# Attention with a bias on one core: ones column on GpSimd, a half-clock term in the emission planner, E tiles of twelve banks, and products of four banks

## The chip, the cores and the metric

The kernel runs on 1 core of a Trainium2 chip. The metric is the device time of one execution in microseconds (us); the number given for a kernel is the median over runs. Engines are named as in the profile: PE is TensorE (PEld its weight loads), DVE is VectorE, ACT is ScalarE, POOL is GpSimd, SP is SyncE.

## The reference

Batch 4, 8 heads, 1024 positions, head dimension 64, all float32, with one bias matrix of 1024 x 1024 for all heads:

```
scores = q @ k^T / sqrt(64) + bias
attn   = softmax(scores, axis=-1)        # denominator + 1e-8
out    = attn @ v
```

The inputs are small (normal draws times 0.1), so the kernel takes no maximum before the exponential.

## The kernel before

**Splitting the exponential.** exp(s + bias) is computed as exp(s) times exp(bias). ACT makes `eb` = exp(bias) once, from a bias transposed on PE (`b_fill`, L138, and `b_exp`, L143), and exp(s) for every head (`s_exp`, L130, into `E` tiles in bf16). DVE multiplies `E` by `eb` in place (`mul_pair`, L148). PE then multiplies the product with V (`av_bank`, L160). V has a 65th column of ones for every head and key block, in the tile `vall`, so that the same matmul gives the softmax denominator; the ones are written once, by a DVE memset (L200). An evacuation takes a reciprocal (L170) and scales (L171), and for the second half of the queries the output DMA follows on the SP queue (L174).

**The unit of work is a bank**: 128 keys by 512 queries of one head, one PSUM bank of scores. There are 16 pairs of heads, each with 2 query halves (`qh`), 8 key blocks (`kc`) and 2 heads: 512 banks, in this order, with the two heads of a pair alternating:

```python
banks = [(pr, h, qh, kc) for pr in range(NP) for qh in range(2) for kc in range(NCH) for h in range(2)]
slots = [[0], [1, 2]] + [list(range(i, min(i + 3, NB))) for i in range(3, NB, 3)]
```

A slot is what one exp instruction takes: 1, then 2, then 3 banks each, and 2 in the last. `s_fill` (L125) is the matmul of a slot, into one of two PSUM buffers of three banks (`ps_s`); so a fill can start when the exp two places earlier is done. Two more PSUM buffers (`ps_x`, tags xa and xb) serve the transposes of K and Q (L88, copied out by DVE at L101 and L97) and the accumulators of the V matmuls. A product of one key block covers the same `eb` block for the two heads. `E` tiles hold 6 banks, and there are 12 of them.

**The order of the work** is written out by a planner in Python. `order` fixes the sequence of ACT: the score slots, with four bias slots put in. For PE and DVE the planner keeps a model clock for each engine (`t_act`, `t_pe`, `t_dve`) with fixed costs in ns, `EXP` and `EXP0` for an exp, `QK` for a score matmul, `AV` for a bank of the V matmul, `TP` for eight transposes, `MUL` for a product, `COPYQ`, `COPYK` and `EVAC` for the other DVE work, and `SEM` for a hand-over, and emits whichever instruction its model has ready first. `pe_pick` lets other PE work go ahead of a fill only if it ends before a limit. The planner starts at the model time `T0`; what lies before (loads, the first transposes, slots 0 and 1) is written by hand. Engines run their instructions in the order in which they were emitted.

**The start.** SP and ACT load the first K chunks (`k0f`) and the first query half (`q0f`) in float32 by four small DMAs. POOL issues the other loads: the second halves of K and Q of pair 0, the first half of the bias, then V of pair 0 (L80, which waits for the ones memset because it writes the same tile), K and Q of pair 1 (L74, L75), the second half of the bias (L203), V of pair 1, and so on. PE is kept busy by six matmuls on zeros (L209). `k_first` (L213 cast, L217 transposes, L218 copy) and `q_first` (L221 cast, L224, L225) prepare the first K chunks and the first query half. After slot 2 the planner puts the transposes of the other K half and of the other query half of pair 0 (L88).

Of the kernel before, what the change touches and what calls it, by code (L numbers as in the profile page):

```python
# [11 lines left out]
ALU = mybir.AluOpType  # L12
# [3 lines left out]
def kernel(  # L16
# [15 lines left out]
    nc = tc.nc  # L32
    B, H, S, D = q.shape
    P = 128
    NCH = S // P
    D1 = D + 1
    NP = B * H // 2
    scale = 1.0 / (D ** 0.5)
    HQ = S // 2
# [8 lines left out]
    consts = ctx.enter_context(tc.tile_pool(name="consts", bufs=1))  # L48
    raw = ctx.enter_context(tc.tile_pool(name="raw", bufs=3))
    kvp = ctx.enter_context(tc.tile_pool(name="kvp", bufs=3))  # L50
    ep = ctx.enter_context(tc.tile_pool(name="ep", bufs=12))
    op = ctx.enter_context(tc.tile_pool(name="op", bufs=2))
    small = ctx.enter_context(tc.tile_pool(name="small", bufs=4))
    ps_s = ctx.enter_context(tc.tile_pool(name="ps_s", bufs=2, space=bass.MemoryType.PSUM))
# [5 lines left out]
    eb = consts.tile([P, 2, NCH, HQ], BF)  # L60
    mask = consts.tile([P, 2, HQ], BF)
    vall = consts.tile([P, 2 * NP, NCH, D1], BF)
# [42 lines left out]
    banks = [(pr, h, qh, kc) for pr in range(NP) for qh in range(2) for kc in range(NCH) for h in range(2)]  # L105
    NB = len(banks)
    slots = [[0], [1, 2]] + [list(range(i, min(i + 3, NB))) for i in range(3, NB, 3)]
    NS = len(slots)
    ET = 6
    etiles = {}  # L110

    def e_at(b, n):
        if b // ET not in etiles:
            etiles[b // ET] = ep.tile([P, ET, HQ], BF, name="E")
        return etiles[b // ET][:, b % ET:b % ET + n, :]

# [28 lines left out]
    def mul_pair(b, n=2):  # L145
        pr, h, qh, kc = banks[b]
        e = e_at(b, n)
        nc.vector.tensor_tensor(e, e, eb[:, qh, kc:kc + 1, :].to_broadcast([P, n, HQ]), op=ALU.mult)  # L148

    oalls = {}  # L150
    po = {}
# [25 lines left out]
    with tc.manual_schedule():  # L177
# [18 lines left out]
        for t in range(2):  # L196
            nc.vector.memset(qT0[t * D:(t + 1) * D, 1 - t, :HQ], 0.0)
            for u in range(2):
                nc.vector.memset(mask[t * D:(t + 1) * D, u, :], 1.0 if t == u else 0.0)
        nc.vector.memset(vall[:, :, :, D:D1], 1.0)  # L200
        load_v(0)
        load_qk(1)
        nc.gpsimd.dma_start(out=btraw[:, QC:, :], in_=bf_[:, QC:, :])  # L203
# [35 lines left out]

        EXP, EXP0, QK, AV, TP = 427, 45, 216, 170, 350
        MUL, COPYQ, COPYK, EVAC, SEM = 600, 650, 420, 620, 80
        order = [("S", g) for g in range(2, NS)]
        for at, x in ((5, (0, 0)), (7, (0, 4)), (11, (1, 0)), (13, (1, 4))):
            order.insert(at, ("B",) + x)
        NO = len(order)
        T0 = 7500.0
        t_act, t_pe, t_dve = T0 + 700, T0, T0 + 500
        filled = []  # L250
        act_end = []
        x_free = {"xa": T0 + 500, "xb": T0}
        x_unit = {}
# [6 lines left out]
        eb_at = {}  # L260
        exp_at = {0: T0, 1: T0 + 700, 2: T0 + 700}
        mul_at = {}
        mul_next = 0
# [9 lines left out]
            return banks[b][:3]  # L273

        dve_q = []

        def cost_act(i):
            item = order[i]
# [2 lines left out]
        def act_end_of(i):  # L281
            if i < 0:
                return T0
            if i < len(act_end):
                return act_end[i]
            return max(t_act, filled[i] + SEM if i < len(filled) else 0) + sum(
                cost_act(j) for j in range(len(act_end), i + 1))

        def pe_fill():
            i = len(filled)  # L290
            if i >= NO or i - 2 >= len(act_end):
                return None
            ready = act_end_of(i - 2) + SEM
            item = order[i]
            if item[0] == "S":
                for b in slots[item[1]]:
                    pr, h, qh, kc = banks[b]
                    for key in ((pr, 1, kc // QC), (pr, 0, qh)):
                        if key not in piece_end:
                            return None  # L300
                        ready = max(ready, piece_end[key] + SEM)
                cost = QK * len(slots[item[1]])
            else:
                ready = max(ready, bias_at[item[1]])
                cost = 2 * TP + 250

            def emit(t):
                if item[0] == "S":
                    s_fill(item[1])
                else:  # L310
                    b_fill(item[1], item[2])
                filled.append(t + cost)
            return ready, cost, emit

        def pe_piece():
            if not pieces:
                return None
            pr, which, half = pieces[0]
            if pr not in raw_at or pr not in raws:
                return None  # L320
            i = min(len(filled), NO - 1)
            while order[i][0] != "S":
                i -= 1
            at = slots[order[i][1]][0]
            if at < (pr - 2) * 32 + 8:
                return None

            left = NCH - av_next % NCH
            busy = x_unit.get(unit_of(av_order[av_next])) if av_next % NCH else None
            tags = sorted((x_free[x], x) for x in x_free if x != busy)  # L330
            if busy and left < 4 and at < pr * 32 - 16:
                return None
            if not busy and av_next and at < pr * 32 - 16 and tags[0][0] + SEM < t_pe and len(tags) > 1 and tags[1][0] > t_pe:
                return None
            free, tag = tags[0]
            ready = max(free + SEM, raw_at[pr][1 - which])

            def emit(t):
                pieces.pop(0)
                copy = transpose_pe(pr, which, half, tag)  # L340
                cost = COPYK if which else COPYQ
                x_free[tag] = 1e12

                def run(t2):
                    copy()
                    x_free[tag] = t2 + cost
                    piece_end[(pr, which, half)] = t2 + cost
                    if which == 0 and half == 1:
                        if pr + 3 < NP:
                            load_qk(pr + 3)  # L350
                            raw_at[pr + 3] = (t2 + 7000, t2 + 7000)
                        if pr + 2 < NP:
                            load_v(pr + 2)
                dve_q.append((t + TP + SEM, 0, cost, run))
            return ready, TP, emit

        def pe_av():
# [23 lines left out]
                    dve_q.append((t + AV + SEM, 1, EVAC, run))  # L381
            return ready, AV, emit

        def pe_pick():
            f = pe_fill()
            best = None
            i = len(filled)
            if f and f[0] <= t_pe:
                return (max(t_pe, f[0]),) + f[1:]
            limit = 1e12  # L390
            if f:
                limit = max(f[0], act_end_of(i - 1) - f[1] - 100)
            elif i < NO:
                limit = max(act_end_of(i - 2) + SEM, act_end_of(i - 1) - 750)
            for c in (pe_piece(), pe_av()):
                if c is None:
                    continue
                start = max(t_pe, c[0])
                if start + c[1] > limit:
                    continue  # L400
                if best is None or start < best[0]:
                    best = (start,) + c[1:]
            if f and (best is None or f[0] <= best[0]):
                best = (max(t_pe, f[0]),) + f[1:]
            return best

        def dve_pick():
            nonlocal mul_next
            c = list(dve_q)
            if mul_next < NB:  # L410
                pr, h, qh, kc = banks[mul_next]
                if mul_next + 1 in exp_at and (qh, kc) in eb_at:
                    b = mul_next

                    def run(t):
                        nonlocal mul_next
                        mul_pair(b)
                        mul_at[b] = mul_at[b + 1] = t + MUL
                        mul_next += 2
                    c.append((max(exp_at[b + 1], eb_at[(qh, kc)]) + SEM, 2, MUL, run))  # L420
            if not c:
                return None
            return min(c, key=lambda x: (max(x[0], t_dve + 100), x[1]))
# [7 lines left out]
        while len(act_end) < NO or av_next < NB or dve_q:  # L431
            c = []
            a, d, p = act_pick(), dve_pick(), pe_pick()
            if a:
                c.append((a[0], 0))
            if d:
                c.append((max(t_dve, d[0]), 1))
            if p:
                c.append((p[0], 2))
            t, who = min(c)  # L440
            if who == 0:
                i = a[2]
                item = order[i]
                t_act = t + a[1]
                act_end.append(t_act)
                if item[0] == "S":
                    s_exp(item[1])
                    for b in slots[item[1]]:
                        exp_at[b] = t_act
                else:  # L450
                    b_exp(item[1], item[2])
                    for kc in range(4):
                        eb_at[(item[1], item[2] + kc)] = t_act
            elif who == 1:
                if d in dve_q:
                    dve_q.remove(d)
                t_dve = t + d[2]
                d[3](t)
            else:
                t_pe = t + p[1]  # L460
                p[2](t)


# [28 lines left out]
```

## Time and profile before

| | us |
|---|---|
| median of 13 runs | 254.38 (253.3 to 255.29) |
| the profiled execution, its own time | 254.6 |
| span of its records | 252.8 |
| ACT busy | 239.1 |
| PE busy | 229.0 |
| DVE busy | 226.5 |
| POOL busy | 52.6 |

The span runs from the first to the last recorded instruction of the program; the time of the same execution is 1.8 us longer. Busy time is the union of an engine's records. On ACT and DVE the record of an instruction overlaps with that of the next by about 0.1 us to 0.4 us when they follow back to back, so the spacing of starts, not the mean of one record, is what an instruction costs there.

### The profile page before, as it was taken

How to read it: one execution, taken by the hardware profiler on the slowest of the kernel's cores; microseconds unless marked ns; L12 is line 12 of the kernel's file. 1: busy time of each engine (PE TensorE's matmuls, PEld its weight loads, DVE VectorE, ACT ScalarE, POOL GpSimd, SP SyncE). 2: the span in 40 equal slices, each digit the busy share in tenths (PEclk: the TensorE clock that was granted, in tenths of full speed). 3: DMA queues.
4: the chain of work that ended last, by engine and by line, in shares of the span. 5: the costliest groups of instructions: out<-in, count | busy, mean ns of one | idle time of the engine just before them, and what ended most of it. 6: DMA issues, size and time to landing. Idle time of an engine off the chain costs nothing.

```text
span 252.8 us, 7210 instructions
## 1 busy us (share of the span) xinstructions
PE 229.0 (91%) x3087; PEld 141.5 (56%) x3142; DVE 226.5 (90%) x461; ACT 239.1 (95%) x180; POOL 52.6 (21%) x72
## 2 busy tenths in 40 slices
PE   6769999999999999999999999999999999999982
PEld 2336755556555556565555556565565655555651
DVE  6309799999999999999999999999999999999994
ACT  3699999999999999999999999999999999999970
POOL 6653213513220513013042204034000000000000
PEclk9799999999999999999999999999999999999997
DMA  7999989989291589429196904949020201111112
GB/s 145 177 216 187 192 89 160 108 105 129 54 155 30 108 78 147 67 61 148 31 148 49 181 14 88 125 84 164 8 84 3 83 3 44 44 43 44 47 38 83
DMA packets 47743, 23.79 MB, mean 94 GB/s; under 512 B 34400, under 2 KB 43360, under 8 KB 47456
## 3 DMA queue, kind: packets, MB, share of 16 engines
q0 software_dynamic: 42272, 14.42, 53.3%
q1 hardware_dynamic: 5296, 8.78, 9.5%
q8 instruction: 24, 0.39, 0.7%
q10 hardware_dynamic: 144, 0.13, 0.2%
q14 instruction: 7, 0.06, 0.1%
HBM read 29.36 MB, written 8.39 MB: 149 GB/s over the span
## 4 chain that ended last, share of the span: by engine, by line
PE 45%; ACT 42%; DVE 8%; issue 2%; DMA 1%; ACTq 0%
ACT E L130 39%; PE ps L125 30%; PE po L160 9%; PE px L88 6%; DVE E L148 5%; ACT eb L143 3%; DVE oall L171 1%; DMA q0f<-in_q_dram 1%; DVE qT L97 1%; ACTq L130 0%; DVE rs L170 0%; DVE qT L225 0%; DVE kr L213 0%; DVE qr L221 0%; PE px L224 0%
## 5 line engine op out<-in xcount | busy, mean ns | idle before, releaser
L130 ACT ACTIVATE E<-ps 128x1536 bf16<-128x1536 f32 (+2 forms) x172 | 230.2, 1665 | 3.4 <-PE ps L125 3.4
L148 DVE TENSOR_TENSOR E<-E,eb 128x1024 bf16<-128x1024 bf16 x256 | 163.7, 683 | 8.0 <-ACT eb L143 7.8
L125 PE MATMUL ps<-qT,kT 128*128 128x512 bf16 x457 | 134.1, 380 | 11.9 <-ACT E L130 5.0
L160 PEld LDWEIGHTS <-E 128*128 128x128 bf16 x2048 | 84.5, 97 | 40.2 <-DVE E L148 2.5
L160 PE MATMUL po<-vall,E 128*128 128x65 bf16 x2048 | 96.3, 194 | 2.7 <-DVE E L148 1.3
L125 PEld LDWEIGHTS <-kT 128*128 128x128 bf16 x512 | 45.4, 97 | 42.2 <-issue 10.5
L74 POOL DMA_DIRECT2D kr<-in_k_dram x15 | 10.5, 699 | 98.5 <-PE px L88 95.4
L80 POOL DMA_DIRECT2D vall<-in_v_dram x32 | 28.1, 882 | 6.7 <-DMA btraw<-in_bias_dram 4.0
L171 DVE TENSOR_TENSOR oall<-po,rs 128x256 f32<-128x256 f32 x64 | 27.2, 425 | 2.4 <-DVE rs L170 0.3
L97 DVE TENSOR_TENSOR qT<-px,mask 128x1024 bf16<-128x1024 bf16 x31 | 21.3, 688 | 1.6 <-PE px L88 0.8
L101 DVE COPY kT<-px 128x512 bf16<-128x512 bf16 x31 | 13.1, 424 | 4.8 <-PE px L88 4.1
L170 DVE RECIPROCAL rs<-po 128x4 f32<-128x4 f32 x64 | 11.4, 178 | 3.4 <-PE po L160 3.1
L75 POOL DMA_DIRECT2D qr<-in_q_dram x15 | 10.7, 716 | 14.9 <-PE px L88 14.0
L88 PE MATMUL px<-ident,kr 128*64 128x128 bf16 x248 | 13.1, 227 | 0.3
L88 PE MATMUL px<-ident,qr 128*64 128x128 bf16 x248 | 13.0, 228 | 0.0
L88 PEld LDWEIGHTS <-kr 128*64 128x64 bf16 x248 | 8.1, 110 | 8.7 <-issue 5.2
L88 PEld LDWEIGHTS <-qr 128*64 128x64 bf16 x248 | 8.2, 111 | 7.6 <-issue 7.0
L143 ACT ACTIVATE eb<-pb 128x2048 bf16<-128x2048 bf16 x4 | 7.5, 1882 | 0.0
L138 PE MATMUL pb<-ident,btraw 128*128 128x128 bf16 x64 | 4.6, 225 | 1.8 <-ACT eb L143 1.0
L138 PEld LDWEIGHTS <-btraw 128*128 128x128 bf16 x64 | 4.6, 146 | 2.7 <-issue 2.4
L209 PE MATMUL wm<-zeros 128*128 128x512 bf16 x6 | 2.7, 629 | 1.2 <-DVE zeros L184 1.2
L185 ACT ACT_TABLE_LOAD x1 | 1.3, 1283 | 1.2 <-PEq L476 1.2
(27 smaller groups left out, 12.4 us busy)
## 6 DMA issues: line engine op xcount, KB each, us to landing
out_dram<-oall SPq DMA_DIRECT2D x32, 256.0 KB, 2.4
vall<-in_v_dram POOLq DMA_DIRECT2D x32, 128.0 KB, 6.3
kr<-in_k_dram POOLq DMA_DIRECT2D x15, 256.0 KB, 3.9
qr<-in_q_dram POOLq DMA_DIRECT2D x15, 256.0 KB, 5.5
btraw<-in_bias_dram POOLq DMA_DIRECT2D x2, 1024.0 KB, 11.3
k0f<-in_k_dram SPq DMA_DIRECT2D x2, 128.0 KB, 3.4
q0f<-in_q_dram ACTq DMA_DIRECT2D x1, 128.0 KB, 2.8
q0f<-in_q_dram SPq DMA_DIRECT2D x1, 128.0 KB, 2.7
```

The lines of the kernel that those rows point to most:

```text
L75: nc.gpsimd.dma_start(out=qr.rearrange("p t c d -> p t (c d)"), in_=qf[pr])
L80: nc.gpsimd.dma_start(out=vall[:, 2 * pr + t, :, :D], in_=vf[pr, :, t])
L88: nc.tensor.transpose(px[t * D:(t + 1) * D, c, :], src[:, t, half * QC + c, :], ident[:])
L97: nc.vector.tensor_tensor(dst[:, :, half * HQ:(half + 1) * HQ], px.rearrange("p c q -> p (c q)").unsqueeze(1).to_broadcast([P, 2, HQ]), ma ...
L101: nc.vector.tensor_copy(dst[:, half * QC:(half + 1) * QC, :], px[:])
L125: nc.tensor.matmul(ps[:, j, :], kT[:, kc, :], qT[:, h, qh * HQ:(qh + 1) * HQ], start=True, stop=True)
L130: nc.scalar.activation(e_at(slots[g][0], n), open_ps.pop(("S", g))[:, :n, :], ACTF.Exp, scale=scale)
L143: nc.scalar.activation(eb[:, qh, k0:k0 + 4, :], open_ps.pop(("B", qh, k0))[:, :4, :], ACTF.Exp)
L148: nc.vector.tensor_tensor(e, e, eb[:, qh, kc:kc + 1, :].to_broadcast([P, n, HQ]), op=ALU.mult)
L160: nc.tensor.matmul(acc[:, i, :], e[:, 0, i * P:(i + 1) * P], vall[:, 2 * pr + h, kc, :], start=(kc == 0 and i == 0), stop=(kc == NCH - 1), ...
L170: nc.vector.reciprocal(rs[:], acc[:, :, D:D1])
L171: nc.vector.tensor_tensor(oall[:, qh * QC:(qh + 1) * QC, :], acc[:, :, :D], rs[:].to_broadcast([P, QC, D]), op=ALU.mult)
```

## The change

There are four edits. The memset of the ones column moves from DVE to POOL, where it stands after the first bias load and before the loads of V. The planner gets a time `COLD`, before which its model charges PE twice the cost, a lower `T0`, and a way to emit PE work when nothing else is left (`force`). `E` tiles hold 12 banks, and there are 6 of them. And `mul_pair` can multiply four banks in one instruction: two key blocks by two heads, with `eb` broadcast over the heads; the planner takes it where, in its model, the exp of the fourth bank is done by the time that DVE is free and no copy or evacuation falls due within the next 600 ns.

```diff
-    ep = ctx.enter_context(tc.tile_pool(name="ep", bufs=12))
+    ep = ctx.enter_context(tc.tile_pool(name="ep", bufs=6))
...
-    ET = 6
+    ET = 12
...
     def mul_pair(b, n=2):
         pr, h, qh, kc = banks[b]
         e = e_at(b, n)
-        nc.vector.tensor_tensor(e, e, eb[:, qh, kc:kc + 1, :].to_broadcast([P, n, HQ]), op=ALU.mult)
+        if banks[b + 1][1] == h:
+            nc.vector.tensor_tensor(e, e, eb[:, qh, kc:kc + n, :], op=ALU.mult)
+        elif n == 4:
+            e = e.rearrange("p (c t) q -> p c t q", t=2)
+            nc.vector.tensor_tensor(e, e, eb[:, qh, kc:kc + 2, :].unsqueeze(2).to_broadcast([P, 2, 2, HQ]),
+                                    op=ALU.mult)
+        else:
+            nc.vector.tensor_tensor(e, e, eb[:, qh, kc:kc + 1, :].to_broadcast([P, n, HQ]), op=ALU.mult)
...
-        nc.vector.memset(vall[:, :, :, D:D1], 1.0)
+        nc.gpsimd.memset(vall[:, :, :, D:D1], 1.0)
...
+        COLD = 10500
...
-        T0 = 7500.0
+        T0 = 6700.0
...
+        def pe_cost(t, c):
+            return c * 2 if t < COLD else c
...
-                filled.append(t + cost)
+                filled.append(t + pe_cost(t, cost))
...
-                dve_q.append((t + TP + SEM, 0, cost, run))
+                dve_q.append((t + pe_cost(t, TP) + SEM, 0, cost, run))
...
-        def pe_pick():
+        def pe_pick(force=False):
...
-                limit = max(f[0], act_end_of(i - 1) - f[1] - 100)
+                limit = max(f[0], act_end_of(i - 1) - pe_cost(t_pe, f[1]) - 100)
...
-                if start + c[1] > limit:
+                if start + pe_cost(start, c[1]) > limit and not force:
...
-                if mul_next + 1 in exp_at and (qh, kc) in eb_at:
-                    b = mul_next
+                b = mul_next
+                if b + 1 in exp_at and (qh, kc) in eb_at:
+                    ready = max(exp_at[b + 1], eb_at[(qh, kc)]) + SEM
+                    n = 2
+
+                    if b % 4 == 0 and b + 3 in exp_at and (qh, kc + 1) in eb_at and b + 3 < NB and \
+                            exp_at[b + 3] + SEM <= max(t_dve, ready) and \
+                            all(x[0] > max(t_dve, ready) + MUL for x in dve_q):
+                        n = 4
+                    cost = MUL * n // 2 - 70 * (n // 4)
...
+                        mul_pair(b, n)
+                        for x in range(n):
+                            mul_at[b + x] = t + cost
+                        mul_next += n
...
-                t_pe = t + p[1]
+                t_pe = t + pe_cost(t, p[1])
```

The two heads alternate in `banks`, so the first branch of `mul_pair` is never taken. In the instruction order of the built program, 81 products have four banks and 94 have two, in place of 256 of two. ACT's sequence of exps is unchanged. Near the start, PE's order after slot 2 becomes: the eight transposes of the other K half, slots 3 and 4, the eight transposes of the other query half, slots 5 and 6; before, it was all sixteen transposes and then slots 3 to 6.

## The prediction

> **What bounds the kernel now.** I read the page's busy shares and costliest groups first, then the timeline of the start and of the end, and the table by stage.
>
> ```profile
> PE 229.0 (91%) x3087; PEld 141.5 (56%) x3142; DVE 226.5 (90%) x461; ACT 239.1 (95%) x180; POOL 52.6 (21%) x72
> L130 ACT ACTIVATE E<-ps 128x1536 bf16<-128x1536 f32 (+2 forms) x172 | 230.2, 1665 | 3.4 <-PE ps L125 3.4
> L148 DVE TENSOR_TENSOR E<-E,eb 128x1024 bf16<-128x1024 bf16 x256 | 163.7, 683 | 8.0 <-ACT eb L143 7.8
> ```
>
> Three engines are above 90%, but only ACT never rests: the exps waited 3.4 us in all. The timeline shows where:
>
> ```profile
> 6.20 0.60 ACT L130 ACTIVATE E<-ps 128x512 bf16<-128x512 f32 x1 [1.32 <-PE ps L125]
> 7.79 1.02 ACT L130 ACTIVATE E<-ps 128x1024 bf16<-128x1024 f32 x1 [0.99 <-PE ps L125]
> 8.96 0.64 PE L88 MATMUL px<-ident,kr 128*64 128x128 bf16 x8
> 9.07 1.45 ACT L130 ACTIVATE E<-ps 128x1536 bf16<-128x1536 f32 x1 [0.26 <-PE ps L125]
> 9.39 0.64 PE L88 MATMUL px<-ident,qr 128*64 128x128 bf16 x8
> 11.31 5.48 ACT L130 ACTIVATE E<-ps 128x1536 bf16<-128x1536 f32 x4 [0.79 <-PE ps L125]
> ...
> 30.48 214.62 ACT L130 ACTIVATE E<-ps 128x1536 bf16<-128x1536 f32 x160
> ```
>
> 1.32 + 0.99 + 0.26 + 0.79 is the whole 3.4 us. From 11.31 to 245.10 ACT runs back to back, one three-bank exp each 1.34 us (214.62/160). So the time is a start (to 11.3), a fixed ACT stretch (234) and a tail after ACT (7.7). Only start and tail can be won; inside, anything that makes ACT wait is lost. The tail:
>
> ```profile
> 230.35 14.75 ACT L130 ACTIVATE E<-ps 128x1536 bf16<-128x1536 f32 x11
> 244.82 3.09 DVE L148 TENSOR_TENSOR E<-E,eb 128x1024 bf16<-128x1024 bf16 x5
> 248.31 0.18 DVE L170 RECIPROCAL rs<-po 128x4 f32<-128x4 f32 x1 [0.39 <-PE po L160]
> 249.07 0.42 DVE L171 TENSOR_TENSOR oall<-po,rs 128x256 f32<-128x256 f32 x1
> ```
>
> Five products, of the ten last banks, start at 244.82. The bank pair first in that row had its second exp done at 241.5 (three exps before the end: 1.34 + 1.34 and 0.92 for the last, which has two banks, before 245.10). So DVE is about 3.3 us behind ACT, and its last product ends at 247.91, 2.81 after the last exp. From there to the end of the span it is 4.9 us of V matmuls, evacuation, output DMA and closing.
>
> **The change, part by part.**
>
> *Four-bank products.* Products follow each other at (3.09 - 0.68)/4 = 0.602 us. 1024 elements at two per DVE cycle of 0.96 GHz (VectorE: DVE Perf Modes, mode table, in the Trainium skill) would be 0.533, so 0.069 is fixed per instruction and a four-bank product should take 0.602 + 0.533 = 1.135. No row shows one. Innermost runs stay 512 contiguous bf16 in all operands, as now, so I take 1.135; bounds are 1.07 (no fixed part) and, if the pattern lost its two-per-cycle rate, about 2.2. In the built order 81 products have four banks: 81 x 0.069 = 5.6 us of DVE time. The same page's measured fixed term of about 150 cycles would make it 12.7; the trace's spacing decides. DVE is not the bound, so this is worth only the 3.3 us by which it lags: 5.6 is enough to remove it. The late part of the order agrees: of the last 64 banks 44 are multiplied in pairs, which the planner does where DVE has nothing waiting.
>
> Tail then, by order: a four-bank product of banks 500 to 503 (exp done 3.6 before ACT's end, call the end 0), from -3.56 to -2.43; one evacuation, 0.55 (178 and 425 ns records, overlapping), to -1.88; pair 504 to -1.28; pair 506 waits for its exp at -0.92, -0.88 to -0.28; pair 508 to 0.32; pair 510 to 0.92, record end 1.0. Before it was 2.81. Gain 1.8; bounds 0 (the lag stays) and 2.1 (product straight behind the last exp).
>
> *Order at the start.* Before, all sixteen transposes stood ahead of slot 3 (the PE rows at 8.96 and 9.39). Now eight do; slot 3's third bank still needs the K copy. PE is slow exactly here:
>
> ```profile
> 6.00:8.00 2.00, 1.27 (x9) 0.50 (x9) 1.09 (x3) 0.81 (x2) 2.00 (x3) 0.90 1.13 208
> 8.00:10.00 2.00, 2.00 (x20) 0.99 (x19) 0.36 (x1) 1.74 (x2) 2.00 (x4) 0.50 1.04 209
> 10.00:12.00 2.00, 1.70 (x7) 0.68 (x7) 0.75 (x2) 1.21 (x2) 0.45 (x1) 0.75 1.30 153
> ```
>
> PE is busy for all of 8 to 10 at a granted clock of 0.50. The query transposes that leave the path took 0.43 there (starts 8.96 and 9.39): gain 0.4, slot 3 at 10.9. They return behind slot 4, where ACT has 1.34 of exp to cover 0.43 plus a fill of 0.81. The rule that weighs here is the skill's (TensorE: Matmul & The Clock Gate, Part 1): the gate looks at free-running windows of 3.4 us, so the slow stretch lies elsewhere in other runs. By the row 0.4; where PE is at full clock here the gain is about 0, where slot 2 also falls into a fast window up to 0.9. I take 0.4.
>
> *Ones column on POOL.* DVE loses one memset ahead of the first query cast, which is on the path to slot 0:
>
> ```profile
> 2.62 0.81 DVE L199 MEMSET mask<- 64x256 uint32 x2
> 4.32 0.49 DVE L221 CAST qr<-q0f 128x256 bf16<-128x256 f32 x1 [0.89 <-DMA q0f<-in_q_dram]
> 4.42 0.27 DVE L200 MEMSET vall<- 128x256 bf16 x1
> 4.73 0.28 DVE L221 CAST qr<-q0f 128x256 bf16<-128x256 f32 x1
> 4.99 1.75 POOL L80 DMA_DIRECT2D vall<-in_v_dram  x2 [1.41 <-DVE qr L221]
> 6.22 0.61 DVE L213 CAST kr<-k0f 128x256 bf16<-128x256 f32 x1
> ```
>
> The query data had landed at 3.51 and DVE was idle from 3.43, yet the memset and the cast only started at 4.32 to 4.42. What held them the trace does not say. If it goes with the memset, the second cast ends when its data (3.9) allow, near 4.2 instead of 5.0, and slots 0 to 2 come 0.4 to 0.8 earlier; if it belongs to the cast, 0.1 is won.
>
> Against it: POOL no longer waits from 3.58 to 4.99. Its memset costs about 0.3 (its 128x128 one took 0.20, its 128x1 ones 0.10), then it issues V from about 3.9, beside the query casts. The last row shows the price: a cast of this size takes 0.28 alone (4.73), but 0.61 beside the V issue that ended at 6.74. The skill (SBUF — State Buffer, Who interferes with whom) says that a DVE cast in its two-port mode and GpSimd take a shared port pair for a whole instruction, the other blocking fully. By the rule the cast at 6.22 would end at 6.74 + 0.28 = 7.02; it ended at 6.83. By the row the second query cast loses up to 0.33; by the rule up to 0.88, an issue's length. Net: gain 0.3 taken, bounds -0.6 and 0.8. POOL's later issues move up 1 us, but the transfers stand in one queue behind the bias (issued 2.98, landed 12.3), so nothing lands earlier or later; that half of the bias is used from 15.5 on, the other (landed 21.4) from 24 on, at most 1.7 us sooner now, and both still are there.
>
> *E tiles.* 6 x 12 = 12 x 6 = 72 banks, 32 us of exps; reuse comes in coarser steps, and at worst 61 banks (27 us) separate an exp from the V matmul it waits for. Cost 0; it would bind only if V matmuls ran 27 us late.
>
> The planner's `COLD`, `T0` and `force` show in the order alone, so they are counted there.
>
> Sum: 1.8 + 0.4 + 0.3 = 2.5, less 0.1 for small waits where the four bias slots meet the transposes of pair 1: 254.6 - 2.4 = 252.2. The profiled execution is 0.2 above the median of 254.38, so 252.0.
>
> **The rivals.**
>
> *B, the start gives more* (0.17): the DVE hold goes and slots 1 and 2 finish before the half-clock stretch: 1.0 to 1.7 at the start, 1.8 at the tail, 250.6 to 251.6. For it: the hold ended only with the memset. Against: it may be the cast's.
>
> *C, the start gives nothing* (0.17): port contention eats the reorder, or the clock is full there: tail alone, 252.5 to 253.6.
>
> *D, DVE stays behind* (0.05): a four-bank product saves nothing, so the lag and with it most of the tail stay: 253.7 to 254.9. The 90% of DVE speaks for it.
>
> *E, slower* (0.11): PE stands at a V matmul whose four-bank product is late, with the next fill behind it. A fill starts when the exp two places before is done and takes 0.81, so it is ready 1.34 - 0.04 - 0.81 = 0.49 before ACT needs it. In the new order the nearest product ahead of a fill belongs to the exp three places before (14 times), and four-bank ones to four places (24 times); before it was never under five. A four-bank product is there 1.3 after its exp; four places leave 1.34 x 2 - 1.3 = 1.4, plus 0.49, less about 0.5 for the V matmuls. So from about 1.4 us of DVE lag at such points ACT waits. If each of the 81 held it by 0.05, that is 4.1: 254.4 - 2.4 + 4.1 = 256.1. At one element per cycle (chance 0.03, inside this case) 81 x 1.07 = 87 us more DVE work would far exceed the some 15 us that DVE has to spare.
>
> *A, the forecast* (0.50): 251.4 to 252.6.
>
> **How the numbers follow.** About 0.3% (0.76 us) is what a measurement of this kernel can tell from no change. A, B and C lie below 253.6: 0.84 faster. D and the mild end of E are within 0.3%: 0.05; slower 0.11. The range 250.6 to 253.7 holds A, B and C. The predicted time is A's.
>
> **What would show it.** A four-bank row on DVE near 1.2 us; last product about 1.0 behind the last exp, not 2.8; the exp row now at 11.31 starting at 10.9 or before; ACT without a gap from there. Wrong if a gap of ACT named after PE ps appears behind the start, if the four-bank row shows over 1.3, or if the query casts end no earlier than 5.0.

## The result, and the profile after

The changed kernel takes 252.58 us (median of 11 runs, 251.62 to 253.22); the kernel before, timed beside it, 254.58 (median of 48). The ratio is 0.9922, 95% interval 0.9905 to 0.994: 2.0 us faster, where 2.4 was forecast. The profiled execution is the median one, 252.58, with a span of 250.8.

From the page of the changed kernel, the exps and the two kinds of product (busy us, mean ns of one, and idle time before them):

```profile
L130 ACT ACTIVATE E<-ps 128x1536 bf16<-128x1536 f32 (+2 forms) x172 | 230.1, 1683 | 3.1 <-PE ps L125 3.1
L152 DVE TENSOR_TENSOR E<-E,eb 128x2048 bf16<-128x2048 bf16 x81 | 97.7, 1217 | 1.7 <-ACT E L130 1.1
L155 DVE TENSOR_TENSOR E<-E,eb 128x1024 bf16<-128x1024 bf16 x94 | 62.3, 684 | 1.6 <-ACT E L130 1.3
```

The exps wait 3.1 us in all, all of it at the start again. Products now wait for exps, 2.4 us in all; before, 7.8 of the products' 8.0 us of waiting was for the exps of the bias. DVE is no longer behind. The tail, from the timeline:

```profile
231.52 13.38 ACT L130 ACTIVATE E<-ps 128x1536 bf16<-128x1536 f32 x10
241.33 1.23 DVE L152 TENSOR_TENSOR E<-E,eb 128x2048 bf16<-128x2048 bf16 x1 [0.24 <-ACT E L130]
244.02 1.90 DVE L155 TENSOR_TENSOR E<-E,eb 128x1024 bf16<-128x1024 bf16 x3 [0.31 <-ACT E L130]
```

The last exp ends at 244.90 (231.52 + 13.38) and the last product at 245.92: 1.02 behind, where it was 2.81. From there to the end of the span it is 4.9, as before. The start:

```profile
3.52 1.65 DVE L228 CAST qr<-q0f 128x256 bf16<-128x256 f32 x2
3.54 1.28 POOL L207 MEMSET vall<- 128x256 bf16 x1
5.12 1.75 POOL L80 DMA_DIRECT2D vall<-in_v_dram  x2 [0.30 <-POOL vall L207]
6.17 0.59 PE L125 MATMUL ps<-qT,kT 128*128 128x512 bf16 x1 [0.32 <-DVE qT L232]
6.79 0.60 ACT L130 ACTIVATE E<-ps 128x512 bf16<-128x512 f32 x1 [1.80 <-PE ps L125]
8.45 1.02 ACT L130 ACTIVATE E<-ps 128x1024 bf16<-128x1024 f32 x1 [1.06 <-PE ps L125]
9.73 6.82 ACT L130 ACTIVATE E<-ps 128x1536 bf16<-128x1536 f32 x5 [0.26 <-PE ps L125]
```

Three things are to be seen. The gap ahead of slot 3 is gone: slots 2 to 6 are one row, and slot 3 starts at 11.07 (9.73 + 1.34). Not all of that is the new order, because the clock was full from 9.7 on. In the profile of e1 (below: the changed kernel but for the memset), with the same order and half clock until 12.0, a gap is left:

```profile
11.56 5.48 ACT L130 ACTIVATE E<-ps 128x1536 bf16<-128x1536 f32 x4 [0.51 <-PE ps L125]
```

There slot 3 starts 1.95 behind slot 2 (9.61), where it was 2.24 in the profile of before (11.31 - 9.07), whose clock was half from 7.6 to 11.0: 0.3 less.

The second thing: the first cast starts at once, at 3.52, but the two end only at 5.17 (5.01 before), and a memset on POOL that I had put at 0.3 took 1.28 beside them. The third: the first score matmul took 0.59, where the same one took 0.38 in the profile of before. PE was at half clock here until 9.7: the five score matmuls from 7.38 took 2.31, the same five in e6, at full clock, 1.25. (The PEclk digit of such a stretch is no help: no change of clock is recorded ahead of it, and it is printed as full.) So slot 0 is 0.6 later than in the profile of before, and the two starts cannot be compared row by row; that needs kernels timed in many executions.

**How the times are read.** Executions of one kernel fall into groups. The table gives the lowest, the median and the highest of each kernel, with the ratio to the runs of before made beside it.

| kernel | lowest | median | highest | ratio, 95% interval |
|---|---|---|---|---|
| before | 253.3 | 254.58 | 255.29 | |
| changed | 251.62 | 252.58 | 253.22 | 0.9922 (0.9905 to 0.994) |
| e1_ones_dve | 251.50 | 252.58 | 253.04 | 0.9932 (0.9908 to 0.9956) |
| e2_two_banks | 252.62 | 253.92 | 254.17 | 0.9983 (0.9962 to 1.0004) |
| e3_old_start | 251.60 | 252.92 | 253.59 | 0.9947 (0.9927 to 0.9968) |
| e4_ones_split | 250.86 | 251.83 | 252.49 | 0.9906 (0.9874 to 0.9938) |
| e6_ones_first_pool | 251.97 | 252.46 | 252.78 | 0.9918 (0.9893 to 0.9942) |
| e7_start_only | 252.49 | 253.56 | 254.05 | 0.9971 (0.9952 to 0.999) |
| e9_split_late_bias | 250.98 | 251.35 | 252.57 | 0.991 (0.9881 to 0.9939) |
| e10_first_late_bias | 251.86 | 252.45 | 252.75 | 0.9934 (0.9909 to 0.996) |

(One execution of before, at 522.17, is left out of its highest. e5 and e8 have one execution each, 252.35 and 254.52.) The profiles suggest what the groups are: the PE clock became full for good at 9.7 us in the changed kernel's (252.58), at 12.0 in e1's (253.04), at 6.1 in e9's (250.98). e6 goes the other way: its profile has full clock from 5.7 and is its slowest (252.78), for a reason given there. The differences below are read from lowest to lowest and highest to highest as well as between medians, in the hope that this compares like with like; that the clock makes the groups was not tested by itself. The intervals of e2 and e7 lie clear of the changed kernel's; those of all the others overlap with it.

### The profile page after: what moved, and what is told of

The parts are those of the page before. It is cut to its first block, busy times and chain, and to the rows that moved or that the text cites. A ratio compares the mean times of both kernels' runs of the same rounds, so it can differ in the third digit from the quotient of the medians.

```text
span 250.8 us, 7098 instructions
## 1 busy us (share of the span) xinstructions
PE 228.1 (91%) x3088; PEld 140.0 (56%) x3142; DVE 221.3 (88%) x379; ACT 239.1 (95%) x180; POOL 53.8 (21%) x73
## 4 chain that ended last, share of the span: by engine, by line
ACT 83%; PE 10%; DVE 3%; issue 2%; DMA 1%; ACTq 0%
ACT E L130 80%; PE ps L125 7%; ACT eb L143 3%; PE po L167 1%; PE px L88 1%; DVE E L155 1%; DMA q0f<-in_q_dram 1%; DVE oall L178 1%; DVE qr L228 1%; DVE qT L232 0%; DVE qT L97 0%; DVE rs L177 0%; PE px L231 0%; PE px L224 0%; DVE kr L220 0%
## 5 line engine op out<-in xcount | busy, mean ns | idle before, releaser
L167 PEld LDWEIGHTS <-E 128*128 128x128 bf16 x2048 | 82.4, 97 | 40.3 <-DVE E L155 4.1
L152 DVE TENSOR_TENSOR E<-E,eb 128x2048 bf16<-128x2048 bf16 x81 | 97.7, 1217 | 1.7 <-ACT E L130 1.1
L167 PE MATMUL po<-vall,E 128*128 128x65 bf16 x2048 | 92.1, 194 | 2.8 <-DVE E L155 1.7
L155 DVE TENSOR_TENSOR E<-E,eb 128x1024 bf16<-128x1024 bf16 x94 | 62.3, 684 | 1.6 <-ACT E L130 1.3
L74 POOL DMA_DIRECT2D kr<-in_k_dram x15 | 10.5, 699 | 95.2 <-PE px L88 91.7
```

What stands on the lines that cost most here:

```text
L152: nc.vector.tensor_tensor(e, e, eb[:, qh, kc:kc + 2, :].unsqueeze(2).to_broadcast([P, 2, 2, HQ]), op=ALU.mult)
L167: nc.tensor.matmul(acc[:, i, :], e[:, 0, i * P:(i + 1) * P], vall[:, 2 * pr + h, kc, :], start=(kc == 0 and i == 0), stop=(kc == NCH - 1), ...
```

## The experiments

### e1: the ones memset back on DVE

```diff
-        nc.gpsimd.memset(vall[:, :, :, D:D1], 1.0)
+        nc.vector.memset(vall[:, :, :, D:D1], 1.0)
```

> The changed kernel with the ones memset back on DVE, all else kept. Theory (the move won nothing, because on POOL the memset of 1.28 us holds the DVE cast beside it for 1.45 us): second query cast ends near 5.0 as in the kernel before (5.17 changed), last exp within 0.2 us of the changed kernel for the same clock at the start, time 252.2 to 252.8, ratio to before 0.991 to 0.994. Rival (the move is what paid): 0.4 to 0.8 us slower than the changed kernel, 253.0 to 253.4. Second rival (the port lock costs the start dearly): 0.4 us or more faster, under 252.2.

Median 252.58, the same as the changed kernel's; lowest and highest are 0.12 and 0.18 lower. Both rivals fall. DVE's start, from the timeline:

```profile
2.62 0.81 DVE L206 MEMSET mask<- 64x256 uint32 x2
4.32 0.50 DVE L228 CAST qr<-q0f 128x256 bf16<-128x256 f32 x1 [0.89 <-DMA q0f<-in_q_dram]
4.43 0.27 DVE L207 MEMSET vall<- 128x256 bf16 x1
4.72 0.29 DVE L228 CAST qr<-q0f 128x256 bf16<-128x256 f32 x1
```

It is the picture of the kernel before, with the casts ended at 5.01. On DVE the memset holds the casts from 3.43; on POOL the first cast starts at 3.52 and stands until POOL's memset is over at 4.82. The move made no gain. By the traces it cost 0.16, the later end of the casts; the times agree with that (0, 0.12 and 0.18), but could not tell it from nothing.

### e2: products of two banks only

```diff
-                    if b % 4 == 0 and b + 3 in exp_at and (qh, kc + 1) in eb_at and b + 3 < NB and \
+                    if False and b % 4 == 0 and b + 3 in exp_at and (qh, kc + 1) in eb_at and b + 3 < NB and \
```

> The changed kernel with products of two banks only (E tiles of 12, start order and POOL memset kept). Theory (the gain is DVE's lag at the end): last product 2.4 to 3.0 us behind the last exp, as before (2.81), in place of 1.02; time 254.2 to 254.7, ratio to before 0.998 to 1.002. Rival (the planner's start terms brought the gain): 252.4 to 253.2, last product within 1.5 us of the last exp.

Median 253.92, 1.0 slower than the changed kernel at the lowest and 0.95 at the highest, 1.3 at the median. The tail, ACT's last exps and DVE:

```profile
230.74 14.75 ACT L130 ACTIVATE E<-ps 128x1536 bf16<-128x1536 f32 x11
245.01 2.49 DVE L155 TENSOR_TENSOR E<-E,eb 128x1024 bf16<-128x1024 bf16 x4
```

The last exp ends at 245.49 and the last product at 247.50: 2.0 behind. Neither the theory nor the rival had that. Without four-bank products the lag comes back by 1.0, not by 1.8, so another part of the change takes 0.8 off it.

### e7 and e8: start terms alone, tiles alone

e7 is the kernel before with `COLD`, `T0 = 6700` and `force`; e8 is the kernel before with `ET = 12` and `bufs=6` for the E tiles.

> The kernel before with the planner's start terms alone (half-clock term, start time 6700, forced emission); two-bank products, E tiles of 6, ones on DVE. Theory (the start terms bring DVE nearer to ACT as well as reordering the transposes): last product 1.9 to 2.1 us behind the last exp, as with two-bank products in the changed kernel (2.01), 0.6 to 1.0 us faster than before: 253.4 to 253.8. Rival (it was the E tiles of twelve banks that took 0.8 off the lag): lag 2.7 to 2.9, time 253.9 to 254.4.

> The kernel before with 6 E tiles of 12 banks alone; the order of every engine is that of before. Theory (the tile size costs and brings nothing): no wait of ACT behind the start, last product 2.7 to 2.9 us behind the last exp. Rival (coarser tiles free the exps of waits or add waits): lag under 2.3, or ACT idle in the middle.

The tail of e7, ACT and DVE:

```profile
230.59 14.75 ACT L130 ACTIVATE E<-ps 128x1536 bf16<-128x1536 f32 x11
244.87 2.49 DVE L155 TENSOR_TENSOR E<-E,eb 128x1024 bf16<-128x1024 bf16 x4
```

e7: last product 2.0 behind, median 253.56, 0.78 under the 254.34 of before beside it; 0.81 under it at the lowest and 1.24 at the highest, which fits 0.8 of tail and 0 to 0.4 of start. e8: last product 2.82 behind, no ACT wait behind the start, DVE's order the same as before, one execution at 254.52. So the other 0.8 are the planner's start terms, and the tiles do nothing by themselves. The four-bank products need them: in tiles of six, banks 4 to 7 would lie in two tiles. A table over the whole run shows what both edits do: for each product I took its start less the end of the exp of its last bank, from the records in order, and averaged over 64 banks (us):

| banks | 0- | 64- | 128- | 192- | 256- | 320- | 384- | 448- |
|---|---|---|---|---|---|---|---|---|
| before | 5.9 | 5.2 | 5.5 | 6.0 | 6.5 | 7.0 | 6.8 | 3.8 |
| e7, start terms alone | 5.6 | 4.8 | 5.0 | 5.4 | 6.0 | 6.4 | 6.4 | 3.3 |
| e3, four banks, old start | 4.4 | 2.5 | 1.7 | 0.6 | 0.9 | 0.6 | 0.6 | 0.3 |
| changed | 4.2 | 0.9 | 1.0 | 0.8 | 0.6 | 0.6 | 0.6 | 0.3 |

The start terms take 0.2 to 0.6 off a lag that then stays for the whole run: DVE with two-bank products only just keeps pace. Which of the places where the start terms change DVE's order does it is not shown. Four-bank products let it catch up by bank 192 even with the old start.

### e3: four-bank products with the old start

```diff
-        COLD = 10500
+        COLD = 0
-        T0 = 6700.0
+        T0 = 7500.0
```

> The changed kernel with the planner's half-clock term off and its start time back at 7500, so that all sixteen transposes stand ahead of slot 3 again. Theory (the reorder is worth 0.4 us where PE is at half clock there): an idle time of ACT of 0.7 to 0.9 us ahead of the exp of slot 3, and 0.3 to 0.8 us slower than the changed kernel: 252.9 to 253.4. Rival (the reorder only moves the wait): the same time within 0.2 us, with no ACT wait at slot 3 or the same wait later.

The last product is 1.01 behind the last exp, as in the changed kernel: four-bank products alone give the whole gain of the tail. The gap ahead of slot 3 is back, but smaller than expected:

```profile
9.72 1.45 ACT L130 ACTIVATE E<-ps 128x1536 bf16<-128x1536 f32 x1 [0.26 <-PE ps L125]
11.46 2.79 ACT L130 ACTIVATE E<-ps 128x1536 bf16<-128x1536 f32 x2 [0.28 <-PE ps L125]
```

In this execution the full clock came at 10.5, just ahead of slot 3's fill. The time is 252.92, 0.34 above the changed kernel at the median, nothing at the lowest (251.60 against 251.62), 0.37 at the highest. That agrees with the forecast's reading of the reorder, 0.4 where PE is at half clock and nothing where it is not, and with the 0.3 read from e1's profile; the intervals of e3 and of the changed kernel overlap.

### e4: the ones pair by pair

```diff
     def load_v(pr):
+        nc.gpsimd.memset(vall[:, 2 * pr:2 * pr + 2, :, D:D1], 1.0)
...
-        nc.gpsimd.memset(vall[:, :, :, D:D1], 1.0)
```

> The changed kernel with the ones written pair by pair on POOL, 16 elements per partition just ahead of that pair's V loads, in place of all 256 at once. Theory (the long memset holds the casts by the shared port): the two query casts end near 4.2 to 4.4 instead of 5.17, slot 0 starts 0.6 to 0.9 us earlier for the same clock, time 251.7 to 252.2. Rival (the casts are held by something else of the start): no earlier than 5.0, time 252.4 to 252.8. Second rival (the V issues, now earlier, lock the port in turn): casts end between 4.6 and 5.2, time 252.2 to 252.6.

```profile
3.55 0.20 POOL L79 MEMSET vall<- 128x16 bf16 x1
3.57 0.65 DVE L228 CAST qr<-q0f 128x256 bf16<-128x256 f32 x2
```

(Rows of POOL and of DVE.) The casts end at 4.22 in place of 5.17, and slot 0's exp starts at 6.24 in place of 6.79, with PE at half clock in both: 0.55, just under what was expected. The time is 251.83; lowest and highest are 0.76 and 0.73 below the changed kernel's. The long memset was what held the casts.

### e5 and e6: the whole memset, away from the casts

e5 puts the whole memset on DVE behind that of the zeros; e6 puts it on POOL behind the identity, ahead of POOL's first load.

> The changed kernel with the whole ones memset on DVE, right behind the memset of the zeros, 2.5 us ahead of the query casts. Theory (256 single bf16 elements, 130 bytes apart, take about 1.27 us to write on either engine, whatever the record says): the next DVE memset starts about 1.2 us behind the ones memset's turn, all later memsets move by 1.2 to 1.3 us, and the first query cast starts at 4.6 to 4.8. Rival (the hold arises between the memset and a cast behind it): the memset takes 0.27 there, the first cast starts at 3.7 to 3.8 and ends by 4.1.

> The changed kernel with the whole ones memset on POOL moved ahead of POOL's first load, behind the identity, where DVE does only memsets. Theory (the memset's 1.28 us are its own, and the cast was held by the shared port): the POOL record is again 1.2 to 1.3 us, DVE's memsets keep their times, the casts end by 4.3, POOL's loads all issue about 1.3 us later and nothing waits for them; time 251.7 to 252.2. Rival (POOL and the cast held each other): the record is 0.3 to 0.4 us here. Second rival (the later loads are missed): ACT waits for the bias near 15 us, time 252.6 or more.

DVE in e5, then POOL and DVE in e6:

```profile
0.90 0.27 DVE L191 MEMSET zeros<- 128x256 uint32 x1
2.04 0.27 DVE L192 MEMSET vall<- 128x256 bf16 x1 [0.87 <-issue]
2.28 0.27 DVE L205 MEMSET qT<- 64x256 uint32 x1
```

```profile
1.26 1.23 POOL L194 MEMSET vall<- 128x256 bf16 x1
3.46 0.29 DVE L228 CAST qr<-q0f 128x256 bf16<-128x256 f32 x1
3.94 0.39 DVE L228 CAST qr<-q0f 128x256 bf16<-128x256 f32 x1 [0.19 <-DMA q0f<-in_q_dram]
```

With no cast near, the memset still takes DVE from 1.17 to 2.31, of which the record shows the last 0.27, and POOL 1.23. Nor was it POOL that held DVE in the kernel before, for POOL did nothing from 3.58 to 4.99 there. So the time is its own: 256 single bf16 elements, 130 bytes apart, on either engine. (The first cast of e5 starts at 4.58, about where the theory had it.) The rival of e5 (a hold between memset and cast) and the first one of e6 fall. In e6 the casts are done at 4.33, and in this execution the full clock came at 5.7. Yet its time is 252.46, no better than the changed kernel. It is the second rival of e6 in kind, a wait of ACT for the bias, though near 25 us and not near 15. ACT's rows:

```profile
25.22 1.88 ACT L143 ACTIVATE eb<-pb 128x2048 bf16<-128x2048 bf16 x1 [0.99 <-PE pb L138]
28.67 1.88 ACT L143 ACTIVATE eb<-pb 128x2048 bf16<-128x2048 bf16 x1 [0.23 <-PE pb L138]
```

PE's transposes there waited for the transfer of the second bias half (0.86 of PE's idle time is put down to it). That half landed at 23.94, where it landed at 21.93 in the changed kernel, although POOL issued it 0.95 earlier (7.32, 8.27). It stands in one queue behind the first half, which was issued 0.63 later (3.61) and landed 1.0 later (13.76); between 5 and 8 us the DMA engines moved 75 to 106 GB/s in e6 and 160 to 228 in the changed kernel. What slowed them is not shown. ACT came to that point 1.2 sooner. What the start won, the bias took back.

### e9 and e10: the second bias slots later

```diff
-        for at, x in ((5, (0, 0)), (7, (0, 4)), (11, (1, 0)), (13, (1, 4))):
+        for at, x in ((5, (0, 0)), (7, (0, 4)), (14, (1, 0)), (16, (1, 4))):
```

e9 puts this on e4, e10 on e6.

> The pair-by-pair ones of e4_ones_split, and the second two bias slots three places later in the sequence of exps (14 and 16 in place of 11 and 13). Theory (where the start is fast, the second bias half, not the start, would hold ACT; at half clock the start still binds): no wait of ACT behind the start in any case, the slowest executions as in e4_ones_split (252.4 to 252.5), the fastest earlier by 0.2 to 0.8 us (250.1 to 250.7), median 251.3 to 251.9; last product still 1.0 behind the last exp. Rival (DVE lacks the second bias half for longer and does not catch up): last product more than 1.5 us behind, or ACT waits for a fill held by a V matmul, time 252.5 or more.

> e6_ones_first_pool with the second two bias slots three places later (14 and 16). Theory (in e6 ACT waited for the transfer of the bias, which POOL issued 0.6 us later): the ACT wait near 25 us is gone and that of about 0.2 us near 15 stays, the executions with an early full clock are 1.0 to 1.5 us faster than e6: 250.6 to 251.5 in place of 252.0 to 252.8. Rival (the wait was for something else behind it, PE or DVE): the same wait two slots later, 252.0 to 252.8.

e9: 251.35, in whose profile ACT never waits from slot 1 on. This is the execution with the full clock from 6.1:

```profile
7.26 7.74 ACT L131 ACTIVATE E<-ps 128x1024 bf16<-128x1024 f32 x6 [0.55 <-PE ps L126]
```

Its highest (252.57) is as expected; its lowest (250.98) is not under e4's (250.86), where 250.1 to 250.7 was expected, so the later bias slots brought nothing that these runs can tell. e10: 252.45, as e6, and its executions miss what was expected. Its profiled execution (251.86) has its last exp at 244.18, 0.87 before that of e6, but the exps that end near 17, 20, 29 and 31 us are still late by 0.15 to 0.26 each. Of PE's idle time 0.6 is still put down to the bias transfer, all of it to the first half (at 13.9). More is put down to the loads of K, which stand in the same queue behind the bias, 0.93 at 16.88 and:

```profile
25.99 0.41 PE L88 MATMUL px<-ident,kr 128*64 128x128 bf16 x8 [0.53 <-DMA kr<-in_k_dram]
```

So e10 took only the second bias half out of the way of the late queue. Why its other executions gained nothing stays open: no trace of them was kept.

Both e4 and e9 are faster than before beyond doubt. That they beat the changed kernel is likely (0.75 from group to group for e4), but their intervals overlap with its own.

## Why the prediction was right, point by point

A row of the changed kernel with two four-bank products back to back:

```profile
22.65 2.35 DVE L152 TENSOR_TENSOR E<-E,eb 128x2048 bf16<-128x2048 bf16 x2
```

- **Four-bank products.** Forecast 1.135 us each; they follow each other at 1.13 in the trace, 0.53 more than a two-bank one, so the two-per-cycle rate held and 0.07 is saved each time. (Two take 2.35 in the row above, and one record 1.22.) The fixed term of 150 cycles that the Trainium skill gives for a single operation (VectorE: DVE Perf Modes, the TRN2 errata) is 156 ns, over twice the 69. It fits the length of a record here (683 - 533 and 1217 - 1067 are both 150 ns), and not the spacing of products back to back.
- **The tail.** Forecast: last product 1.0 behind the last exp, gain 1.8. Measured: 1.02 and 1.79, and e3 and e7 show whose it is. What the sum missed is that the start terms alone would take 0.8 of it; I had counted them for the order at the start only. With both, nothing adds: four-bank products alone reach the lag of 1.0 (e3).
- **The order at the start.** Forecast 0.4 by the row, 0 at full clock. e3 against the changed kernel: 0 to 0.37, 0.34 at the median. The row that was to show it, slot 3 at 10.9 or before, did not come: 11.07, because slot 0 was 0.6 later.
- **The ones column.** Forecast a gain of 0.3; measured a cost of about 0.15 (e1). This is the term that was mis-sized, and its sign was wrong, inside the bounds given. A sign of being wrong that I had named came true: the casts end at 5.17, no earlier than 5.0. I took POOL's memset at 0.3 from a dense memset of 128 elements, and read DVE's record of 0.27 as its cost, although DVE did nothing else from 3.43 to 4.69. It took 1.28, and it held the cast beside it: from 3.52 to 4.97, 0.15 beyond the memset's end. (By the records the cast begins 0.02 ahead of the memset; in e3 it begins 0.12 behind it, and ends at 4.97 as well.) V's loads were issued at 5.12 and not at 3.9. The rule of the Trainium skill (SBUF — State Buffer, Who interferes with whom) that I had weighed down, the other engine blocked for the whole instruction, fits here to 0.13: it would have the cast end at 4.82 + 0.28 = 5.10. Beside POOL's DMA issues it does not fit: such casts took 0.29 to 0.65 in these runs, where 0.28 is the time alone.
- **E tiles.** Forecast nothing; e8 shows nothing.
- **The rivals.** E did not come: ACT has no wait behind the start. D did not come. B did not come either, though its ground was right: the hold belonged to the memset, but the memset took its time along to POOL. C, the start gives nothing, covers the time too (252.5 to 253.6), and is half right: the reorder's 0.34 was paid back in part by the ones column's 0.15.

The terms as measured, 1.8 + 0.34 - 0.15, give 2.0, which is the result; the last two are read from kernels whose intervals overlap, so each of them is rough. So the mechanism of nine tenths of the gain, the tail, was right. That the time still lies inside the forecast's 251.4 to 252.6 is luck: it does so by 0.02, with one start term off by 0.45.

## What to carry to other kernels

An engine at 90% that never stops the bound engine can still set the end, by how far it lags when the bound engine is done: compare the last products with the last exps before counting its instructions. When a record is short but the engine stands idle before it with its data there, the idle time belongs to the instruction until shown otherwise, and it will go along when the instruction is moved. Before an engine's work is moved beside another's, look whether one holds the other; here a part of the work (16 elements of 256) was all that the start needed.

## What the runs showed of the hardware that was not expected

- A memset of 256 bf16 elements, 130 bytes apart, takes 1.23 to 1.28 us on POOL (e6, changed) and 1.15 on DVE (e5), where its record says 0.27; 16 such elements take 0.20 on POOL (e4). By these two, an estimate is 4.3 ns for each further element ((1.23 - 0.20)/240).
- A float32 to bf16 cast on DVE stands for the whole of a POOL memset (1.45 us in place of 0.28, changed kernel), while DVE memsets beside the same POOL memset keep their times (0.27 and 0.49, in e6).
- The point from which PE has its full clock for good lies anywhere from 5.3 to 12.7 us in the profiles of this case, and the times of one kernel spread by up to 2.0 us.
